# A two-layer decoder step in fp32 on one core: resident split weights, queued sums of x, rearranged decode

## The chip, the core and the metric

One core of a Trainium2 chip runs the whole step. Its engines are TensorE (PE in the profile; PEld is its weight load), VectorE (DVE), ScalarE (ACT), GpSimd (POOL) and SyncE (SP, which here only issues DMAs). The metric is the device time of one execution in microseconds (us), the median of the runs.

## The reference

One inference step of a small hybrid decoder, d_model 1024, 1024 prompt tokens and 8 decode tokens, feed-forward width 2816, 8 heads. Layer 0 mixes by a gated short convolution, layer 1 by differential attention (two softmaxes per head, one subtracted from the other) over keys and values of the prompt; the decode tokens also read 256 cached positions through a page table. Everything is fp32.

```python
def trunk(x, ...):
    for l in range(2):
        if l == 0:
            y = short_conv_mixer(x, conv_state, w_in, conv_w, w_mix_out)   # (b * conv(c * h)) @ w_out
        else:
            k, v = x @ w_kv          # rotary on k
            q = x @ w_q              # rotary on q
            o = diff_softmax_attention(q, k, v, ..., lam)   # softmax_1 - lam * softmax_2, times v
            y = (rms_norm(o, subln_g) * (1 - lam_init)) @ w_o
        x = layer_norm(alpha * x + y, ln1_g[l], ln1_b[l])
        x = layer_norm(alpha * x + (silu(x @ w_gate[l]) * (x @ w_up[l])) @ w_down[l], ln2_g[l], ln2_b[l])
```

## The kernel before

Tokens lie along the free dimension, d_model along the 128 partitions in 8 blocks. The 1032 tokens are four chunks of 258 (`HALF` = chunks (0, 1) and (2, 3)). An fp32 matmul is done as three products of rounded halves (hi by hi, lo by hi, hi by lo): `xhf` and `xlf` hold x so split, and a dense block of 128 outputs for one chunk (`dense`) is 24 matmuls of 128x258, eight at L299, eight at L300 and eight at L302.

Weights come from DRAM through a `Stream`: a DMA of 128x512 fp32 into `raw` (L134, on SP), a rounding copy to `whi` on ScalarE (L166), and `wlo` = raw - whi on GpSimd (L167). The ring has four split tiles and four raws; a second stream with 7 and 4 serves q and k. A pass that runs again over other chunks streams and splits its weights again.

Work off TensorE that belongs to a neighbouring stage (LayerNorms, sums of x, the decode) is written as generators on a side queue, `Side`; after each dense block a few steps of the front one are issued. `need(c)` drains the LayerNorm of chunk c where its result is wanted. A scheduler then orders each engine's instructions by its own priorities, so that the queues hold them in other orders than the code.

`layer_norm` (L327 to L367): mean by a matmul with ones (L327), subtraction of it (L338, two of 128x1032), squares on ScalarE (L343), their sum on VectorE (L335), variance by a matmul (L351, `st<-ssq`), square root on ScalarE (L353), reciprocal on VectorE (L354), multiplication (L358, two of 128x1032), scale and shift on ScalarE (L360), and the split into `xhf` (ScalarE, L365) and `xlf` (VectorE, L367). The next dense product of that chunk waits for the last two.

The FFN runs 11 groups of 256 hidden columns. The first is plain; groups 1 to 9 use a Winograd-like scheme with seven products of sums of weights and of sums of x (`sums_of`: `Th`, `Tl`, L318 and L319, called through `split_into`); the last is plain again, over chunks ((0, 1), (2, 3)) in layer 0 and (0, 1), (2), (3) in layer 1. `gate` (L470) and `up` (L478) fill `hidh`/`hidl`; `down` adds its products to the residual (L443, L445) and sums it for the next mean (L451).

After layer 0's FFN come q and k (8 blocks each, in two passes over two chunks; the stores of k are `out_k<-t`), v, and between them the decode: cached keys and values are gathered by indirect DMAs on GpSimd (L805), multiplied on VectorE (keys L827, L829; values L882, added in pairs L886) and, for values, summed over positions by `od` matmuls (L888). The softmax of the decode starts once chunk 3's keys are there (`k_done`). Then attention per head and block of queries loads k, q and v again from DRAM (`load`, `load_q`, `load_v`: L937 to L956) and takes scores at L969 and L970. The output projection is `project`, with four blocks of chunk 0 begun inside attention, in passes over chunks (0), (1, 2), (3).

## Time and profile before

| | |
|---|---|
| median of 3 runs | 2616.46 us (2613.49 to 2617.38) |
| profiled execution | 2614.26 us, span 2612.5 us |
| mean granted TensorE clock | 0.975 |
| PE busy | 2446.3 us, 94% of the span |
| DVE, POOL, ACT busy | 1502.9, 1315.0, 1015.1 us |

The busy time of an engine counts its instructions, not its waits. TensorE is busy for 94% of the span; the other engines are busy for 58% and less, unevenly. The granted clock is a share of full speed: 1.00 is 2.4 GHz and 0.5 is 1.2 GHz.

### The profile page before, as it was taken

Reading aid. Unit: us, or ns where it says so; the run is one execution under the profiler, and the core shown is the slowest. Engines: PE = TensorE matmul, PEld = TensorE weight load, DVE = VectorE, ACT = ScalarE, POOL = GpSimd, SP = SyncE. Lnnn points to the kernel's source line nnn. Section 1 sums busy time; section 2 is a strip of 40 time slices with the busy share of each in tenths; the row PEclk is TensorE's granted clock in tenths of the full one; section 3 lists DMA queues with packets and bytes.
Section 4 is the critical chain, followed back from the end, with each engine's and each line's share of the span. In section 5 each row is a group of like instructions: output and inputs, shape, how many; then the busy total and the mean of one; then the engine's idle time right before and its main releaser. Section 6 shows DMA issues by size and latency. Waiting matters only on the chain. (4 is left out here: it accounts for less than half of the span.)

```text
span 2612.5 us, 49681 instructions
## 1 busy us (share of the span) xinstructions
PE 2446.3 (94%) x19482; PEld 2381.7 (91%) x19482; DVE 1502.9 (58%) x2808; ACT 1015.1 (39%) x2248; POOL 1315.0 (50%) x1111
## 2 busy tenths in 40 slices
PE   9999998999999999989879899898799999999995
PEld 8999998999999999979849898797799999999984
DVE  4333878555555554594782677768654444444467
ACT  4213456322222222454322677646422222222234
POOL 4224576655555554465572244457555555555443
PEclk9999998999999999999989999999899999999997
DMA  4113242211111112267982768343211111111232
GB/s 158 49 45 93 82 139 84 63 49 50 53 50 49 49 49 86 90 224 225 290 281 92 194 179 242 107 140 106 77 57 50 49 49 49 50 50 49 82 94 97
DMA packets 158618, 266.16 MB, mean 102 GB/s; under 512 B 17672, under 2 KB 60072, under 8 KB 157232
## 3 DMA queue, kind: packets, MB, share of 16 engines
q1 hardware_dynamic: 151168, 236.01, 29.9%
q0 software_dynamic: 4608, 16.78, 1.8%
q10 hardware_dynamic: 2608, 10.20, 1.2%
q8 instruction: 153, 2.51, 0.4%
q14 instruction: 81, 0.66, 0.1%
HBM read 219.53 MB, written 43.39 MB: 101 GB/s over the span
## 5 line engine op out<-in xcount | busy, mean ns | idle before, releaser
L167 POOL TENSOR_TENSOR wlo<-raw,whi 128x512 fp32r<-128x512 f32 x570 | 773.2, 1369 | 760.6 <-ACT whi L166 496.2
L299 PE MATMUL mm<-xhf,whi 128*128 128x258 f32 x3200 | 809.9, 288 | 50.2 <-ACT xhf L365 19.8
L300 PE MATMUL mm<-xlf,whi 128*128 128x258 f32 x3200 | 804.1, 286 | 9.7 <-DVE xlf L367 9.0
L299 PEld LDWEIGHTS mm<-xhf,whi 128*128 128x128 f32 x3200 | 613.4, 192 | 60.7 <-ACT xhf L365 20.7
L300 PEld LDWEIGHTS mm<-xlf,whi 128*128 128x128 f32 x3200 | 614.2, 192 | 13.1 <-DVE xlf L367 10.4
L166 ACT CAST whi<-raw 128x512 fp32r<-128x512 f32 x570 | 349.5, 619 | 652.7 <-PE mm L300 499.0
L302 PE MATMUL mm<-xhf,wlo 128*128 128x258 f32 x3200 | 478.7, 285 | 4.0 <-POOL wlo L167 4.0
L302 PEld LDWEIGHTS mm<-xhf,wlo 128*128 128x128 f32 x3200 | 426.3, 191 | 5.7 <-POOL wlo L167 5.2
L299 PE MATMUL mm<-hidh,whi 128*128 128x258 f32 x1408 | 366.3, 288 | 14.6 <-DVE g L478 3.5
L300 PE MATMUL mm<-hidl,whi 128*128 128x258 f32 x1408 | 374.6, 286 | 2.8 <-DVE hidl L319 2.8
L302 PE MATMUL mm<-hidh,wlo 128*128 128x258 f32 x1408 | 282.8, 284 | 1.4 <-POOL wlo L167 1.4
L299 PEld LDWEIGHTS mm<-hidh,whi 128*128 128x128 f32 x1408 | 264.1, 190 | 19.2 <-DVE rf L445 5.3
L300 PEld LDWEIGHTS mm<-hidl,whi 128*128 128x128 f32 x1408 | 268.1, 191 | 6.4 <-DVE hidl L319 6.4
L167 POOL TENSOR_TENSOR wlo<-ws,whi 128x512 fp32r<-128x512 f32 x108 | 139.2, 1289 | 209.3 <-ACT whi L166 209.3
L299 PE MATMUL mm<-Th,whi 128*128 128x258 f32 x864 | 219.0, 285 | 4.7 <-DVE m L506 4.7
L302 PEld LDWEIGHTS mm<-hidh,wlo 128*128 128x128 f32 x1408 | 221.0, 192 | 1.6 <-POOL wlo L167 1.6
L300 PE MATMUL mm<-Tl,whi 128*128 128x258 f32 x864 | 217.4, 282 | 0.0
L445 DVE TENSOR_TENSOR rb<-mm,rb 128x258 f32<-128x258 f32 x320 | 134.6, 425 | 99.2 <-PE mm L302 99.1
L445 DVE TENSOR_TENSOR rf<-mm,rf 128x258 f32<-128x258 f32 x352 | 142.8, 422 | 68.7 <-PE mm L302 68.6
L299 PEld LDWEIGHTS mm<-Th,whi 128*128 128x128 f32 x864 | 163.9, 190 | 6.8 <-DVE m L506 6.5
L300 PEld LDWEIGHTS mm<-Tl,whi 128*128 128x128 f32 x864 | 163.6, 189 | 0.0
L166 ACT CAST whi<-ws 128x512 fp32r<-128x512 f32 x108 | 66.9, 620 | 229.9 <-PE mm L300 208.6
(221 smaller groups left out, 3717.7 us busy)
## 6 DMA issues: line engine op xcount, KB each, us to landing
raw<-in_wts SPq DMA_DIRECT2D x570, 256.0 KB
qh<-qh SPq DMA_DIRECT2D x64, 128.0 KB
ql<-ql SPq DMA_DIRECT2D x64, 128.0 KB
rf<-in_xT SPq DMA_DIRECT2D x16, 258.0 KB
stash<-rf SPq DMA_DIRECT2D x4, 1032.0 KB
qh<-hi SPq DMA_DIRECT2D x32, 129.0 KB
ql<-lo SPq DMA_DIRECT2D x32, 129.0 KB
out_k<-t SPq DMA_DIRECT2D x32, 129.0 KB
```

The costliest lines, as they stand in the source:

```text
L166: nc.scalar.copy(out=hi, in_=src)
L167: g.tensor_tensor(out=lo, in0=src, in1=hi.bitcast(F32), op=ALU.subtract)
L299: T.matmul(ps, lhsT=wh, rhs=h, start=(first and i == 0), stop=False, **kw)
L300: T.matmul(ps, lhsT=wh, rhs=l, start=False, stop=False, **kw)
L302: T.matmul(ps, lhsT=wl, rhs=h, start=False, stop=(last and i == len(terms) - 1), **kw)
L445: V.tensor_tensor(out=R[:, n], in0=ps, in1=R[:, n], op=ALU.add)
```

## The change

Four things. First, weights that a stage uses over several passes are split once and stay on chip (`Resident`): the output projection's eight blocks, in passes over single chunks, and of the last FFN group both gates, both ups and half of the downs, in the space of `T`, which is closed before it; layer 0's last group now has layer 1's order, and in both the first gate of chunk 3 goes ahead of chunk 2's downs. Second, the splits of the sums of x are queued behind the last LayerNorm's copies on ScalarE and VectorE, and the LayerNorm's reciprocal is written to PSUM. Third, the first two q blocks use the main stream, the second stream has 8 split tiles and 3 raws, and keys go over chunk 3 first and then over the other three; the decode's od products are issued one pair late, and its gathers behind them. Fourth, attention's first loads are issued on GpSimd.

```diff
+class Resident:
+
+    RAWS = 4
+
+    def __init__(self, nc, wts, pool, keys):
+        self.nc, self.wts, self.pool, self.keys, self.tiles = nc, wts, pool, keys, []
+        self.raws = deque()
+        self.loaded = 0
+        self._load()
+
+    def _load(self):
+        while len(self.raws) < self.RAWS and self.loaded < 2 * len(self.keys):
+            raw = self.pool.tile([P, 512], F32, tag="rraw", name="rraw", bufs=self.RAWS)
+            self.nc.sync.dma_start(out=raw, in_=self.wts[UIDX[self.keys[self.loaded // 2]], self.loaded % 2])
+            self.raws.append(raw)
+            self.loaded += 1
+
+    def get(self, key):
+        i = 2 * self.keys.index(key)
+        while len(self.tiles) < min(2 * len(self.keys), i + 6):
+            hi, lo = (self.pool.tile([P, 512], F32R, name=f"res{n}{len(self.tiles)}") for n in "hl")
+            raw = self.raws.popleft()
+            self.nc.scalar.copy(out=hi, in_=raw)
+            self.nc.gpsimd.tensor_tensor(out=lo, in0=raw, in1=hi.bitcast(F32), op=ALU.subtract)
+            self.tiles.append((hi, lo))
+            self._load()
+        return self.tiles[i:i + 2]
+
+
...
-    def pair():
+    def pair(key=None):
+
+        for res in kept.values():
+            if key in res.keys:
+                return res.get(key)
...
+    order = {}
...
-        V.reciprocal(out=ssq, in_=ssq)
+        V.reciprocal(out=var, in_=ssq)
...
-            V.tensor_tensor(out=v, in0=v, in1=ssq.unsqueeze(1).broadcast_to([P, KP, CH]), op=ALU.mult)
+            V.tensor_tensor(out=v, in0=v, in1=var.unsqueeze(1).broadcast_to([P, KP, CH]), op=ALU.mult)
...
+                order["A"] = A.copy(out=xh[c][:, ks], in_=v).ins
+                order["V"] = V.tensor_tensor(out=xl[c][:, ks], in0=v, in1=xh[c][:, ks].bitcast(F32),
+                                             op=ALU.subtract).ins
...
-                split_into(h[:, i], l[:, i], u)
+                with tc.issue_after(order["A"]), tc.issue_after(order["V"]):
+                    split_into(h[:, i], l[:, i], u)
...
+            blocks = pair(("down", l, g, i)) if ("down", l, g, i) in final else None
             for _ in range(2):
-                w = ws.take()
+                w = blocks[_] if blocks else ws.take()
...
-        def plain(g, chunks):
-            for f in (2 * g, 2 * g + 1):
-                block(half(("gate", l, f)), lambda f=f: gate(f, chunks))
-                block(half(("up", l, f)), lambda f=f: up(f, chunks))
+        final = [(n, l, f) for f in (NF - 2, NF - 1) for n in ("gate", "up")] + [("down", l, NG - 1, 0)]
+
+        def keep_final():
+            tpool.close()
+            kept["ffn"] = Resident(nc, wts, tpool.enter_context(tc.tile_pool(name="kept", bufs=1)), final)
+
+        def needs(*keys):
+            return half(*[k for k in keys if k not in final])
+
+        def plain(g, chunks, some=slice(0, 4)):
+            todo = [(n, f) for f in (2 * g, 2 * g + 1) for n in (gate, up)]
+            for n, f in todo[some]:
+                block(needs((n.__name__, l, f)), lambda n=n, f=f: n(f, chunks))
 
         def downs(g, chunks, ln=None):
             for i in range(2):
-                block(half(("down", l, g, i)), lambda i=i: down(g, i, chunks, ln))
+                block(needs(("down", l, g, i)), lambda i=i: down(g, i, chunks, ln))
 
...
+                block([], keep_final)
             downs(g, range(NCH))
-        for chunks in (((0, 1), (2,), (3,)) if l else HALF):
-            plain(NG - 1, chunks)
-            downs(NG - 1, chunks, (1, l, l == 1))
+        ln = (1, l, l == 1)
+        g = NG - 1
+        plain(g, (0, 1))
+        downs(g, (0, 1), ln)
+        plain(g, (2,))
+        plain(g, (3,), slice(0, 1))
+        downs(g, (2,), ln)
+        plain(g, (3,), slice(1, 4))
+        downs(g, (3,), ln)
 
 
...
+        def total(b):
+            for half in range(2):
+                T.matmul(od[half], lhsT=sel[:, b], rhs=vv[2 * b % 8][:, half * 512:(half + 1) * 512],
+                         start=(b == 0), stop=(b == DEC - 1))
+
         for j, (b, pg) in enumerate(pairs):
-            if j + ahead_v < 16:
-                gather(vv[(j + ahead_v) % 8], cache_v, *pairs[j + ahead_v])
             t = vv[j % 8].rearrange("p (h e) -> p h e", e=VD)
             V.tensor_tensor(out=t, in0=t, in1=at[:, pg, b].unsqueeze(2).broadcast_to([P, HEADS, VD]), op=ALU.mult)
             yield
             if pg:
                 t0 = vv[(j - 1) % 8]
                 V.tensor_tensor(out=t0, in0=t0, in1=vv[j % 8], op=ALU.add)
-                for half in range(2):
-                    T.matmul(od[half], lhsT=sel[:, b], rhs=t0[:, half * 512:(half + 1) * 512],
-                             start=(b == 0), stop=(b == DEC - 1))
+                if b:
+                    total(b - 1)
+                for i in range(j + 5, min(j + 7, 16)):
+                    gather(vv[i % 8], cache_v, *pairs[i])
                 yield "op"
+        yield "op"
+        total(DEC - 1)
         yield "op"
...
-        load(0)
-        load_q(0, 0)
-        load_v(0)
+        load(0, G)
+        load_q(0, 0, G)
+        load_v(0, G)
...
-            w = pair() if n not in begun or 0 not in chunks else None
+            w = pair(("o", n)) if n not in begun or 0 not in chunks else None
...
-        for chunks in ((0,), (1, 2), (3,)):
+        for c in range(NCH):
             for n in range(KT):
-                block([] if 0 in chunks and n < BEGIN else half(("o", n)), lambda n=n, chunks=chunks: f(n, chunks))
+                block([], lambda n=n, c=c: f(n, (c,)))
 
 
...
-        open_pools(stack, ("big", 1, {}), ("m", 8, {}), ("g", 2, {}))
+        nonlocal tpool
+        open_pools(stack, ("hid", 1, {}), ("m", 8, {}), ("g", 2, {}))
+        pools["hid"] = [pools["hid"].tile([P, 2, NCH, CH], F32R, name=f"hid{n}") for n in "hl"]
+        tpool = stack.enter_context(ExitStack())
+        open_pools(tpool, ("big", 1, {}))
         pools["T"] = [pools["big"].tile([P, 2, 3, KP, CH], F32R, name=f"T{n}") for n in "hl"]
-        pools["hid"] = [pools["big"].tile([P, 2, NCH, CH], F32R, name=f"hid{n}") for n in "hl"]
 
...
-    produce("k", (HALF[1], HALF[0]))
+    early_q, part_q = part_q[:2], part_q[2:]
+    produce("k", ((3,), (0, 1, 2)))
...
+            run(early_q)
+            ws = Stream(nc, wts, pools["wb"], items(part_q, part_k), 8, 3)
...
-        ffn_space(ph)
         rb = pools["r"].tile([P, NCH, KT, CH], F32, name="rb")
         for c in range(NCH):
             r[c] = rb[:, c]
         reload(None)
+        with ExitStack() as pw:
+            open_pools(pw, ("wo", 1, {}))
+            kept["o"] = Resident(nc, wts, pools["wo"], [("o", n) for n in [*range(BEGIN, KT), *range(BEGIN)]])
+            run(part_o)
+        kept.clear()
+        ffn_space(ph)
```

VectorE in layer 0, where the last LayerNorms of the convolution mixer meet the sums of x. The first piece is the kernel before; `Tl` is the low half of a sum of x, `ssq` the sum of squares and later its square root, `st` the mean in PSUM.

```order
L335 TENSOR_TENSOR ssq<-ssq,t 128x258
L319 TENSOR_TENSOR Tl<-m,Th 128x258
L451 TENSOR_TENSOR sum<-sum,rf 128x258
L319 TENSOR_TENSOR Tl<-m,Th 128x258 x7
L354 RECIPROCAL ssq<-ssq 128x258
L319 TENSOR_TENSOR Tl<-m,Th 128x258 x2
L338 TENSOR_TENSOR rf<-rf,st 128x1032 x2
L358 TENSOR_TENSOR rf<-rf,ssq 128x1032 x2
L319 TENSOR_TENSOR Tl<-m,Th 128x258 x2
```

The same place of the changed kernel, on VectorE, and, after the cut, the row at which the last LayerNorm ends and what follows it.

```order
L373 TENSOR_TENSOR ssq<-ssq,t 128x258
L491 TENSOR_TENSOR sum<-sum,rf 128x258
L392 RECIPROCAL st<-ssq 128x258
L376 TENSOR_TENSOR rf<-rf,st 128x1032 x2
L396 TENSOR_TENSOR rf<-rf,st 128x1032 x2
...
L405 TENSOR_TENSOR xlf<-rf,xhf 128x4x258 x2
L354 TENSOR_TENSOR Tl<-m,Th 128x258 x3
```

The `Tl` splits have left the place ahead of chunk 2's reciprocal and chunk 3's subtraction of the mean, and stand behind the last copies of chunk 3.

TensorE in layer 1, from the variance of chunk 3's LayerNorm (`st<-ssq`) to the gate of chunk 3 (`mm<-xhf` just behind it before the change). First the kernel before.

```order
L302 MATMUL mm_22605<-xhf,wlo 128x258 x8
L351 MATMUL st<-ssq,cs 128x258
L299 MATMUL mm<-xhf,whi 128x258
L299 MATMUL mm_22605<-xhf,whi 128x258
L300 MATMUL mm<-xlf,whi 128x258
```

The changed kernel on TensorE, from the same product on: the blocks `mm_22178` (24 matmuls), `mm_22179` (24), `mm` (chunk 2's gate, 24) and `mm_22450` (24), and then chunk 3's gate in the last two rows.

```order
L389 MATMUL st<-ssq,cs 128x258
L334 MATMUL mm_22178<-xhf,whi 128x258
...
L337 MATMUL mm_22178<-xhf,wlo 128x258 x8
...
L337 MATMUL mm_22179<-xhf,wlo 128x258 x8
...
L337 MATMUL mm<-xhf,wlo 128x258 x8
...
L337 MATMUL mm_22450<-xhf,wlo 128x258 x8
L334 MATMUL mm<-xhf,whi 128x258
L335 MATMUL mm<-xlf,whi 128x258
```

Before, no matmul stands between the variance and chunk 3's gate; now 96 do.

SyncE's DMA queue just ahead of attention, before the change: stores of v, and the first loads of k (`tk`), q (`qh`, `ql`) and v (`tv`).

```order
L739 DMA out_v<-dec_v 8x256
L736 DMA out_v<-vt 128x256 x7
L937 DMA tk<-kh 64x1024
L736 DMA out_v<-vt 128x256
L938 DMA tk<-kl 64x1024
L937 DMA tk<-kh 64x1024
L938 DMA tk<-kl 64x1024
L950 DMA qh<-qh 64x512 x2
L950 DMA ql<-ql 64x512 x2
```

The same loads after the change, on GpSimd, behind the last weight splits and the decode's scaling.

```order
L167 TENSOR_TENSOR wlo<-raw,whi 128x512 x12
L974 TENSOR_SCALAR ss<-ss 8x8
L975 TENSOR_TENSOR ss<-ss,mhalf 8x8
L1001 DMA tk<-kh 64x1024
L1002 DMA tk<-kl 64x1024
L1001 DMA tk<-kh 64x1024
L1002 DMA tk<-kl 64x1024
L1014 DMA qh<-qh 64x512 x2
L1014 DMA ql<-ql 64x512 x2
```

The thirteen loads have moved from SyncE's queue to GpSimd's, where nothing else stands between them.

## Rows read from the trace of the kernel before

**Rows 1.** The page, group five: busy, mean, then idle before it and why.

```profile
L299 PE MATMUL mm<-xhf,whi 128*128 128x258 f32 x3200 | 809.9, 288 | 50.2 <-ACT xhf L365 19.8
```

**Rows 2.** Windows, PE: length, busy (matmuls), granted clock, DMA share, GB/s.

```profile
200.00:240.00 40.00, 40.00 (x336) 1.00 0.33 93
400.00:440.00 40.00, 28.53 (x201) 0.83 0.24 73
1120.00:1160.00 40.00, 29.87 (x204) 0.87 0.72 241
1280.00:1320.00 40.00, 32.09 (x248) 0.91 1.00 347
1840.00:1880.00 40.00, 28.27 (x190) 0.76 0.26 80
2560.00:2600.00 40.00, 23.21 (x143) 0.79 0.25 86
```

**Rows 3.** Timeline of DVE, 388 to 396 us, LayerNorms of chunks 2 and 3.

```profile
388.99 5.16 DVE L319 TENSOR_TENSOR Tl<-m,Th 128x258 fp32r<-128x258 f32 x7
394.07 1.75 DVE L354 RECIPROCAL ssq<-ssq 128x258 f32<-128x258 f32 x1
```

**Rows 4.** Timeline of PE, 405 to 440 us.

```profile
426.90 0.80 PE L299 MATMUL mm<-xhf,whi 128*128 128x258 f32 x2 [8.35 <-ACT xhf L365]
```

**Rows 5.** Timeline of PE, 1837 to 1849 us.

```profile
1837.18 0.70 PE L351 MATMUL st<-ssq,cs 128*128 128x258 f32 x2 [1.11 <-DVE ssq L335]
1848.15 0.80 PE L299 MATMUL mm<-xhf,whi 128*128 128x258 f32 x2 [10.27 <-ACT xhf L365]
```

**Rows 6.** Timeline of PE, 1688 to 1722 us.

```profile
1703.33 0.36 PE L299 MATMUL mm<-xhf,whi 128*128 128x258 f32 x1 [1.97 <-DVE xlf L1046]
```

**Rows 7.** Timeline of PE, 1100 to 1180 us.

```profile
1123.35 0.60 PE L351 MATMUL st<-ssq,cs 128*128 128x258 f32 x2
1130.04 0.58 PE L299 MATMUL mm<-xhf,whi 128*128 128x258 f32 x1 [6.09 <-ACT whi L166]
1137.33 0.51 PE L299 MATMUL mm<-xhf,whi 128*128 128x258 f32 x2 [1.18 <-ACT xhf L365]
```

**Rows 8.** Lines L358 and L338: durations min/median/max in ns, first and last start.

```profile
L358 DVE TENSOR_TENSOR rf<-rf,ssq x16: 1216/1232/2324, 304.9 to 1184.0; 128x1032 f32<-128x1032 f32 x16
...
L338 DVE TENSOR_TENSOR rf<-rf,st x16: 1215/1222/1230, 289.0 to 1169.7; 128x1032 f32<-128x1032 f32 x16
```

**Rows 9.** Timeline of PE and ACT, 1280 to 1362 us.

```profile
1295.74 0.58 PE L299 MATMUL mm<-xhf,whi 128*128 128x258 f32 x1 [5.71 <-ACT whi L166]
1336.03 3.57 PE L888 MATMUL od<-rf,sel 128*8 128x512 f32 x4 [10.46 <-DVE rf L886]
...
1294.76 0.41 ACT L318 CAST hi<-t 128x258 fp32r<-128x258 f32 x1 [9.17 <-DMA out_k<-t]
```

**Rows 10.** Timeline of DVE, 1324 to 1334 us.

```profile
1324.58 5.22 DVE L882 TENSOR_TENSOR rf<-rf,at 128x1024 f32<-128x1024 f32 x3
1332.40 1.21 DVE L886 TENSOR_TENSOR rf<-rf 128x1024 f32<-128x1024 f32 x1
```

**Rows 11.** Timelines of SP, POOL and PE about the first loads of attention.

```profile
1432.77 0.51 SPq L937 DMA_DIRECT2D tk<-kh  x1
1437.09 1.23 SPq L950 DMA_DIRECT2D ql<-ql  x2
...
1286.80 0.96 POOL L805 DMA_INDIRECT rf<-in_cache_k,idx  x1 [0.16 <-DVE dec_k L680]
...
1443.49 0.55 PE L969 MATMUL S<-tk,qh 128*128 128x256 f32 x1 [5.78 <-DMA ql<-ql]
```

**Rows 12.** Timeline of PE, 2535 to 2612 us.

```profile
2544.57 0.39 PE L299 MATMUL mm<-hidh,whi 128*128 128x258 f32 x1 [3.49 <-DVE g L478]
2575.56 0.39 PE L299 MATMUL mm<-hidh,whi 128*128 128x258 f32 x1 [1.93 <-ACT whi L166]
2591.90 1.20 PE L412 MATMUL st<-sum,cs 128*128 128x258 f32 x2 [5.74 <-DVE sum L451]
```

23 lines of the change are left out of this document (12 added, 11 removed).

## The prediction

> **What bounds the kernel now.** I read the page's list of costly groups first. A matmul of a dense product is recorded at 288 ns because matmuls are pipelined; the largest cause of PE's idle time before such a line is the ScalarE copy of a LayerNorm's result, xhf [rows 1]. Then I cut the span into 40-us windows. An undisturbed window holds 336 matmuls, so one costs 40/336 = 0.119 us, and each matmul missing from a window of dense products is 0.119 us lost. Most windows are full, so nothing that merely saves work on another engine can be gained there. The losses stand where one stage ends and the next begins: 16.1 us in 400 to 440 (135 matmuls missing), 15.7 in 1120 to 1160, 10.5 in 1280 to 1320, 17.4 in 1840 to 1880, 23.0 in 2560 to 2600 [rows 2]. Part of each is waiting and part a lower granted clock behind the wait: in 1840 to 1880 PE was idle for 40 - 28.27 = 11.7 us, so the other 5.7 us of the loss is slow matmuls at a mean clock of 0.76 [rows 2]. I then read, for each of these places, what PE waited for in its timeline.
>
> **The change, part by part.**
>
> *O projection into FFN1.* Before, the mean-square product of chunk 3's LayerNorm starts at 1837.18 and the gate of chunk 3 is the very next work on PE; it starts at 1848.15, after 10.27 us of waiting for xhf [rows 5]. So the chain from the variance to xhf takes 10.97 us, all uncovered. The new project() goes chunk by chunk, so chunks 1 and 2 are normalised earlier, and the order of PE shows 96 matmuls between that same product and the gate of chunk 3: 96 x 0.119 = 11.4 us of cover. Covered work on VectorE and ScalarE gets into the chain, though (gates and ups of chunks 0 to 2). I take a remaining wait of 2 us: 9 us gained, and 5 of the 5.7 us of slow clock and smaller waits about it. Term: 14 us gained; bounds 6 (chain lengthened to 17 us) and 17.4 (the whole loss of that window).
>
> *Convolution mixer into FFN0.* Before, VectorE does seven Tl splits for 5.16 us ahead of the reciprocal of chunk 2's LayerNorm [rows 3], and everything of chunk 3's LayerNorm queues behind it; PE then waits 8.35 us for chunk 3's xhf [rows 4]. After, all Tl splits stand behind the last LayerNorm's copies, so this chain begins 5 us earlier. What is late next: the splits themselves, needed only by the first FFN group of sums, a full pass of gate and up later. PE reaches the gate no earlier, so at most 8.35 us and the slow clock behind it (16.1 - 11.5 idle = 4.6 us) can go. Term: 6 gained; bounds 3 (ScalarE, which the splits also leave, was not in the way) and 12.
>
> *LayerNorm's reciprocal in PSUM.* The product with the reciprocal reads PSUM instead of SBUF. The same shape with a PSUM operand (L338) never takes over 1.23 us; with an SBUF operand (L358) the median is the same and the longest 2.32 [rows 8]. So it is worth nothing at the median and up to 1.1 us per instruction where something is in the way. It is already in the terms of the chains.
>
> *FFN0 into q.* Before, PE waits 6.09 us for the first weights of a stream whose buffers become free only with the last FFN matmul, then 1.18 us for xhf of chunk 1; that arrives at 1137.33, 14.0 us after the variance product at 1123.35 [rows 7]. After, the first two q blocks come from the main stream, whose weights are there. But chunk 0's 24 matmuls cover 2.9 us of the 14, and chunk 1's first matmul stands next on PE, ahead of chunk 0's second block. The same chain then ends the same stall. Term: 2 gained; bounds -2 and 6 (the weights' wait).
>
> *Keys and decode.* The od products wait 10.46 us [rows 9]: five multiplications by the softmax are issued on VectorE ahead of the first addition that od needs, at 5.22/3 = 1.74 us each, and the addition takes 1.21 [rows 10]. After, four stand ahead and about 40 matmuls (4.8 us) stand on PE between the softmax's transposition and the first od pair; the second group of three pairs, 18 matmuls later, again waits for three more pairs. I sum 4 x 1.2 + 1.2 + 0.5 - 4.8 = 2 us for the first and about 6 for the second: 2 to 3 us gained. Against it: the first key pass now has one chunk, so it needs two weight tiles of 256 KB per 24 matmuls (2.86 us) where it had 48, in a stretch where the DMA share is 1.00 at 347 GB/s [rows 2]. The 5.71 us that PE waited there for whi came from a ScalarE queue held 9.17 us by an out_k transfer [rows 9]; the later pass of three chunks asks for less. Term: 4 gained; bounds -10 (that wait twice more) and 10.5 (the window's loss).
>
> *Attention's first loads, from SP to POOL.* Before, SP issues the first tk at 1432.77 and the eighth load it needs ends its issue at 1438.32: 0.6 us each, one store among them; the first scores start at 1443.49 after 5.78 us of waiting [rows 11]. In the new order the first load waits for the same matmul, so it cannot start earlier. No plain load issued by POOL is in the trace; the nearest row is a gather, 0.96 us [rows 11]: 8 x 0.96 = 7.7 us, 2 us later than SP. Term: 2 lost; bounds 0 (landing, not issue, sets the end) and 5 lost (all 13). The Trainium skill, "DMA: Bandwidth & Descriptors", Specifications and "SWDGE vs HWDGE vs iDMA", puts the first byte of a GpSimd-issued DMA at about 1 us and of one from SP at about 0.6, and says plain loads belong on SP: by that 8 x 0.4 = 3.2 us would be lost here and the sum come out 1.2 us worse. No row here shows a plain load issued by POOL, so the trace neither bears it out nor contradicts it.
>
> *O projection's start.* The resident weights lie where attention's tiles lay, and their first load waits for the last transposition of attention, the matmul just ahead of the first that needs them. Before, the stream was already full and PE only waited 1.97 us, until 1703.33, for xlf [rows 6]. The nearest row of a cold start is the 6.09 us above [rows 7]: 1701.36 + 6.1 = 1707.5, so 4.1 later. Term: 4 lost; bounds 2 and 8. That 32 fewer splits follow in the later passes is hidden beneath PE's full windows and worth nothing.
>
> *FFN's last group and the end.* The gate of chunk 3 ahead of chunk 2's downs puts 24 matmuls (2.9 us) over a wait of 3.49 us, and the resident weights take away 1.93 [rows 12]. But in the new order chunk 1's normalisation ends only beside the last matmuls, so two products of 1.2 and a reciprocal of 1.75 [rows 3, 8] move to the queue ahead of chunk 3's sums, for which PE waits 5.74 [rows 12]. Term: 3 gained; bounds -2 and 7.
>
> Sum: 14 + 6 + 2 + 4 - 2 - 4 + 3 = 23 us. The profiled execution took 2614.26 us with a span of 2612.5, 2.2 below the median of the runs; 2616.5 - 23 = 2593.
>
> **The rivals.**
> *The chains take the stall's place* (20%). LayerNorm's chain is limited by VectorE, whose queue holds the same work in another order; the wait for chunk 3's xhf would come back elsewhere. For it: the sums of squares, splits and multiplications still have to run on it in the same 40 us. Against it: 96 matmuls of cover. Then the two first terms shrink to their lower bounds, 6 + 3 instead of 20: 12 us gained in all, less the 4 that the decode may not give: 8, 2608.
> *The key pass is bound by DMA* (14%, slower). In its one-chunk pass: 16 weight tiles of 256 KB (4.2 MB), some ten gathers and five broadcasts of 512 KB (7.9 MB), 24 stores of 129 KB (3.2 MB), 15.3 MB at the 347 GB/s that the window shows [rows 2] is 44 us against 8 x 24 x 0.119 = 22.9 us of matmuls. If none of it is loaded ahead or let run behind, PE waits 21 us and runs at a lower clock afterwards, about 6: 27 lost instead of 4 gained, 2593 + 31 = 2624. It decides from about 23 + 4 = 27 us lost in this pass. Against it: most weights of the pass are in the ring before it begins, and before the change the same crowding cost 10.5 us.
> *All chains covered* (11%). The upper bounds of the first two terms and of the end: 17.4 + 12 + 7 instead of 23 adds 13: 2580, and down to 2570 where the keys' window empties too.
>
> **How the numbers follow.** 55% for the sum above, whose own range is 2580 to 2606 (the terms' bounds taken as independent). The other cases reach from 2570 to 2624; leaving out the outer half of the first and most of the slower one, 2570 to 2616 holds 8 in 10. A measurement of this kernel tells about 0.2%, 5.2 us, from no change. Faster: 55 + 11 + 10 of the 20 of the stalled case: 76%. The same: the rest of that, 10%, and 1 of the slower case: 11%. Slower: 13%.
>
> **What would show it.** Right: no wait of 8 us or more for xhf at the gate of chunk 3 in either FFN; a wait for a resident weight of some 4 to 6 us at the first o projection matmul; the first scores no earlier after the last v product than now; an xhf wait of about 10 us at the second q product. Wrong: a new wait for whi or wlo in the first key pass of over 10 us in all; a wait for Tl or Th in the first group of sums; chunk 3's final sum more than 6 us after the last down product.

## The result and the profile after

The changed kernel takes 2587.52 us (median of 4 runs, 2584.38 to 2593.24) against 2615.97 for the kernel before, run beside it: ratio 0.9895 (95% interval 0.9875 to 0.9914, in brackets from here on), so 28.5 us faster where 23 were forecast. The profiled executions compare in the same way, span 2582.6 against 2612.5 us. The two kernels have the same 19482 matmuls, so the n-th of each can be set side by side. This ledger is made of their start times, in us from the start of the span, in one trace of each.

| stretch (n-th matmul) | before, us | after, us | gained | forecast |
|---|---|---|---|---|
| to 4000: convolution mixer, start of FFN0 | 513.6 | 513.1 | 0.6 | 6 |
| to 8700: FFN0 | 1084.2 | 1085.2 | -1.5 | 0 |
| to 9350: FFN0's last group, first q blocks | 1183.7 | 1186.8 | -2.1 | 2 |
| to 10700: q, keys, decode | 1387.9 | 1389.3 | 1.6 | 4 |
| to 12000: start of attention | 1567.1 | 1577.5 | -8.9 | -2 |
| to 12750: attention | 1685.4 | 1694.3 | 1.5 | 0 |
| to 12900: start of the output projection | 1706.6 | 1720.2 | -4.8 | -4 |
| to 14200: output projection into FFN1 | 1906.8 | 1888.7 | 31.8 | 14 |
| to 18700: FFN1 | 2467.4 | 2449.9 | -0.7 | 0 |
| to the last: FFN1's last group and the end | 2599.6 | 2569.2 | 12.9 | 3 |

The sum is nearly right, but six of its seven terms are not. A stretch differs from trace to trace even where no edit touches it: over the kernels below, from the 9350th to the 10700th matmul by -2.2 to 2.0 us against the kernel before, from the 12900th to the 14200th by 29.7 to 31.8. Differences of two or three us between single traces tell nothing.

The page's line of the commonest product, and then PE in windows (length, busy, matmuls, granted clock, DMA share, GB/s), as in [rows 1, 2]:

```profile
L334 PE MATMUL mm<-xhf,whi 128*128 128x258 f32 x2720 | 686.3, 287 | 40.3 <-ACT xhf L403 20.5
```

```profile
1320.00:1360.00 40.00, 27.77 (x159) 0.83 0.72 250
1440.00:1480.00 40.00, 26.65 (x158) 0.79 0.73 175
1760.00:1800.00 40.00, 40.00 (x330) 1.00 0.08 28
1800.00:1840.00 40.00, 39.39 (x325) 1.00 0.29 86
1840.00:1880.00 40.00, 34.58 (x261) 0.96 0.23 73
```

Two windows of the kernel before that belong beside them:

```profile
1760.00:1800.00 40.00, 35.96 (x287) 1.00 0.47 143
1800.00:1840.00 40.00, 28.60 (x200) 0.90 0.24 74
```

and the longest wait in them, from PE's timeline:

```profile
1821.79 0.58 PE L299 MATMUL mm<-xhf,whi 128*128 128x258 f32 x1 [4.41 <-ACT g L470]
```

The three windows from 1760 held 287, 200 and 190 matmuls [rows 2]; after, the first two are full and the third has 261. That is the gain. 1440 to 1480 held 233 before and holds 158: attention's first scores wait longer. In 1120 to 1160, with 204 before [rows 2] and 210 after, little has changed. What PE waits for most after, in total (times, longest):

```profile
PE mm L334 <- ACT xhf L403: 20.5, 2, 11.9
PE mm L337 <- POOL wlo L167: 13.7, 2, 11.7
```

Of the waits for xhf the one of 10.27 us at FFN1's gate [rows 5] is gone, the one at FFN0's gate has stayed, and the one at q has grown from 1.18 [rows 7] to 11.89. One of 11.67 for wlo is new, and the first scores wait 8.13 instead of 5.78 [rows 11]. Where they stand on PE's timeline (start, length, instruction, then in brackets the wait and its releaser; from seven places of the trace):

```profile
424.27 0.80 PE L334 MATMUL mm<-xhf,whi 128*128 128x258 f32 x2 [8.64 <-ACT xhf L403]
...
454.34 0.39 PE L334 MATMUL mm<-hidh,whi 128*128 128x258 f32 x1 [1.85 <-DVE rf L483]
...
1137.65 0.80 PE L334 MATMUL mm<-xhf,whi 128*128 128x258 f32 x2 [11.89 <-ACT xhf L403]
...
1341.50 1.66 PE L337 MATMUL mm<-xhf,wlo 128*128 128x258 f32 x6 [11.67 <-POOL wlo L167]
...
1447.30 0.55 PE L1033 MATMUL S<-tk,qh 128*128 128x256 f32 x1 [8.13 <-issue]
1454.26 0.55 PE L1034 MATMUL S<-tk,ql 128*128 128x256 f32 x1 [3.58 <-DMA ql<-ql]
...
1715.12 0.58 PE L334 MATMUL mm<-xhf,resh 128*128 128x258 f32 x1 [4.87 <-ACT resh L203]
...
2558.87 0.99 PE L389 MATMUL st<-ssq,cs 128*128 128x258 f32 x2 [3.59 <-DVE ssq L373]
2568.63 1.23 PE L464 MATMUL st<-m,cs 128*128 128x258 f32 x2 [7.91 <-DVE m L462]
```

*FFN0's gate of chunk 3* waits 8.64 us, as before (8.35, [rows 4]). The variance product ahead of it starts at 413.00 after and 415.60 before, so the chain from there to xhf takes 11.3 us in both. ScalarE and VectorE show what it consists of:

```profile
414.35 1.28 ACT L391 ACT_TABLE_LOAD   x1
415.64 0.48 ACT L391 ACTIVATE ssq<-st,eps_t 128x258 f32<-128x258 f32 x1
...
419.23 4.05 ACT L398 ACTIVATE rf<-rf,prm_t 128x258 f32<-128x258 f32 x8 [1.41 <-DVE rf L396]
...
416.15 1.77 DVE L392 RECIPROCAL st<-ssq 128x258 f32<-128x258 f32 x1 [1.16 <-ACT ssq L391]
417.96 2.37 DVE L396 TENSOR_TENSOR rf<-rf,st 128x1032 f32<-128x1032 f32 x2
```

A table load, the square root, the reciprocal, a multiplication, eight scalings and a copy: each waits for the one before it, and no split of sums stands among them. Moving the splits let this chain start 2.6 us earlier and did not shorten it. Nor did the start hold: at the 3400th matmul the changed kernel is 3.6 us ahead of the kernel before, and between the 3500th and the 3525th, in FFN0's first downs, it gives 2.9 back. The downs wait there for VectorE's additions to the residual (1.85 us above, none before), and the moved splits stand in VectorE's queue among them:

```profile
451.38 1.17 DVE L354 TENSOR_TENSOR xlf<-m,xhf 128x258 fp32r<-128x258 f32 x1
```

The kernel below whose splits are not queued has no such wait there.

*The second q product* waits 11.89 us; only chunk 0's 24 matmuls of the first q block stand on PE while chunk 1's chain runs. VectorE is busy for 19.86 of the 20 us from 1120 to 1140, and ScalarE, which needs 4.2 us to scale the chunk, stands in its queue behind copies of weights that have not landed:

```profile
1128.97 1.93 ACT L166 CAST whi<-raw 128x512 fp32r<-128x512 f32 x3 [2.79 <-DMA raw<-in_wts]
1130.81 2.08 ACT L398 ACTIVATE rf<-rf,prm_t 128x258 f32<-128x258 f32 x4
```

*The od products* no longer show a wait for VectorE [rows 9], but the dense product ahead of them waits 11.67 us for a wlo, and VectorE has finished by then. POOL has that split behind a gather, and the gather stands there while VectorE multiplies and adds:

```profile
1330.63 9.53 POOL L862 DMA_INDIRECT rf<-in_cache_v,idx  x1 [5.96 <-DVE rf L947]
1340.18 1.27 POOL L167 TENSOR_TENSOR wlo<-raw,whi 128x512 fp32r<-128x512 f32 x1
...
1338.11 1.21 DVE L947 TENSOR_TENSOR rf<-rf 128x1024 f32<-128x1024 f32 x1
```

VectorE's last addition ends at 1338.11 + 1.21 = 1339.32, and the gather at 1330.63 + 9.53 = 1340.16, 0.84 later. Before, the gather at this place took 8.39 us, but four splits had been made between it and the gather ahead of it, not two, and PE waited for a split only 2.79 us:

```profile
1333.88 8.39 POOL L805 DMA_INDIRECT rf<-in_cache_v,idx  x1 [6.30 <-DVE rf L886]
```

*Attention's first loads*, now on POOL (start, length, instruction, wait and releaser):

```profile
1434.45 0.64 POOL L1001 DMA_DIRECT2D tk<-kh  x1 [14.92 <-PE vps L788]
1440.75 0.52 POOL L1014 DMA_DIRECT2D qh<-qh  x1 [2.03 <-DMA tk<-kh]
1442.18 0.52 POOL L1014 DMA_DIRECT2D qh<-qh  x1 [0.91 <-DMA tk<-kl]
1445.93 0.52 POOL L1014 DMA_DIRECT2D ql<-ql  x1 [1.21 <-DMA tk<-kl]
```

Issuing one takes 0.52 to 0.64 us, about as long as on SP (0.51, and 1.23 for two, [rows 11]). But the ninth to twelfth each wait until one of the first four has landed, and SP, free meanwhile, sends loads for later blocks past them.

### The profile page after: what moved, and what is told of

It reads as the page before. It is cut to its first block, busy times and chain, and to the rows that moved or that the text cites. A ratio compares the mean times of both kernels' runs of the same rounds, so it can differ in the third digit from the quotient of the medians.

```text
span 2582.6 us, 49334 instructions
## 1 busy us (share of the span) xinstructions
PE 2435.3 (94%) x19482; PEld 2374.2 (92%) x19482; DVE 1457.1 (56%) x2808; ACT 981.6 (38%) x2194; POOL 1233.4 (48%) x1072
## 5 line engine op out<-in xcount | busy, mean ns | idle before, releaser
L167 POOL TENSOR_TENSOR wlo<-raw,whi 128x512 fp32r<-128x512 f32 x482 | 643.7, 1344 | 689.1 <-ACT whi L166 516.7
L334 PE MATMUL mm<-xhf,whi 128*128 128x258 f32 x2720 | 686.3, 287 | 40.3 <-ACT xhf L403 20.5
L335 PE MATMUL mm<-xlf,whi 128*128 128x258 f32 x2720 | 682.3, 285 | 1.4 <-DVE xlf L354 0.8
L334 PEld LDWEIGHTS mm<-xhf,whi 128*128 128x128 f32 x2720 | 520.2, 191 | 47.5 <-ACT xhf L403 20.9
L335 PEld LDWEIGHTS mm<-xlf,whi 128*128 128x128 f32 x2720 | 520.4, 191 | 4.1 <-issue 1.7
L166 ACT CAST whi<-raw 128x512 fp32r<-128x512 f32 x482 | 296.4, 619 | 592.0 <-PE mm L335 406.0
L337 PE MATMUL mm<-xhf,wlo 128*128 128x258 f32 x2720 | 409.4, 285 | 13.7 <-POOL wlo L167 13.7
L337 PEld LDWEIGHTS mm<-xhf,wlo 128*128 128x128 f32 x2720 | 364.1, 192 | 16.8 <-POOL wlo L167 14.2
L334 PE MATMUL mm<-hidh,whi 128*128 128x258 f32 x1344 | 350.5, 286 | 12.9 <-DVE g L518 2.3
L335 PE MATMUL mm<-hidl,whi 128*128 128x258 f32 x1344 | 355.1, 285 | 1.7 <-DVE hidl L354 1.3
```

Source lines behind the costliest of these rows:

```text
L166: nc.scalar.copy(out=hi, in_=src)
L167: g.tensor_tensor(out=lo, in0=src, in1=hi.bitcast(F32), op=ALU.subtract)
L334: T.matmul(ps, lhsT=wh, rhs=h, start=(first and i == 0), stop=False, **kw)
L335: T.matmul(ps, lhsT=wh, rhs=l, start=False, stop=False, **kw)
L337: T.matmul(ps, lhsT=wl, rhs=h, start=False, stop=(last and i == len(terms) - 1), **kw)
```

## The experiments

All are timed beside the kernel before; stage times are taken from one trace of each, as in the ledger. Kernels not said to differ are the changed kernel with one edit.

**Attention's first loads back on SP.**

```diff
-        load(0, G)
-        load_q(0, 0, G)
-        load_v(0, G)
+        load(0)
+        load_q(0, 0)
+        load_v(0)
```

> The changed kernel with attention's first thirteen loads given back to SP. In the changed kernel's trace each of POOL's plain loads takes 0.53 to 0.64 us to issue, no more than SP's 0.6, but the ninth to twelfth wait 2.03, 0.91, 1.51 and 1.21 us for the landing of the first four, while SP sends loads for later heads past them; PE waits 8.13 us for the first scores and 3.58 us for the next query tile. Theory A (that wait in POOL's queue, and SP's later loads let through, cost the 6 us which the profile lost here): back on SP the waits are about 5.8 and 0.4 us as before, the time is 2582 us, ratio to before 0.987. Rival B (issue on POOL costs 2 us, as predicted): 2585.5 us, ratio 0.9884. Rival C (bandwidth sets the end of these loads on either engine): 2587.5 us, ratio 0.9891 to 0.9895, and a wait of 8 us again.

Measured: 2582.43 us, ratio 0.9862 [0.9845, 0.9879]. The first scores wait for loads by SP:

```profile
1449.01 0.55 PE L1033 MATMUL S<-tk,qh 128*128 128x256 f32 x1 [6.39 <-DMA ql<-ql]
```

From the 11000th to the 12000th matmul this kernel loses 0.7 us against the kernel before. The changed kernel loses 9.2 there; in the seven kernels below that keep POOL's loads, 7 to 13. Theory A holds, and the edit makes the kernel faster: the interval just touches that of the changed kernel, but the stage shows it, and a kernel below with the same loads has 0.9861. Whether POOL's waits or the loads that pass them cost the time was not separated.

**The order of the projection alone**, in the kernel before:

```diff
-        for chunks in ((0,), (1, 2), (3,)):
+        for chunks in ((0,), (1,), (2,), (3,)):
```

> The kernel before with one edit: the output projection's passes take chunks 0, 1, 2, 3 one at a time instead of 0, (1, 2), 3; the weights are streamed and split anew in each pass. Theory A (the order alone covers the LayerNorm chains, since two splits of 1.34 us on POOL just fit into 24 matmuls of 2.86 us): no wait over 3 us for xhf at the gate of chunk 3, and 20 to 31 us less: 2585 to 2596 us, ratio 0.988 to 0.992. Rival B (residency is what pays: with a pair of tiles for every 24 matmuls the splits on POOL and the copies on ScalarE, which the LayerNorms need too, become the bound of the passes): the wait for xhf goes, waits for wlo and whi take its place, and under 10 us are gained: 2606 to 2617 us, ratio 0.996 to 1.000.

Measured: 2615.93 us, ratio 0.9992 [0.9983, 1.0001]. The long wait for xhf at the gate of chunk 3 is gone, as the order should make it, and other waits have come (the last row is POOL's window):

```profile
1762.02 0.39 PE L299 MATMUL mm<-xhf,whi 128*128 128x258 f32 x1 [3.00 <-ACT whi L166]
...
1817.52 0.55 PE L299 MATMUL mm<-xhf,whi 128*128 128x258 f32 x1 [5.78 <-DVE rb L443]
...
1760.00:1800.00 40.00, 36.13 (x30) 0.91 0.55 153
```

At the 13550th matmul it is 29.7 us behind the kernel before, and by the 14200th it has made up 26 of them. POOL, which splits the weights and makes the sums of x, is busy for 36.13 of 40 us (32.00 before). Rival B holds: order alone is worth nothing.

**Residency without the order**, the old passes from the resident weights:

```diff
-        for c in range(NCH):
+        for chunks in ((0,), (1, 2), (3,)):
             for n in range(KT):
-                block([], lambda n=n, c=c: f(n, (c,)))
+                block([], lambda n=n, chunks=chunks: f(n, chunks))
```

> The changed kernel with its output projection in the old passes, chunk 0, then 1 and 2 together, then 3, from the resident weights. Theory A (the order covers the chains): the wait of about 10 us for xhf at the gate of chunk 3 returns, with the smaller ones before it, and 10 to 20 us of the 31 gained between the first o product and FFN1 are lost again: 2598 to 2608 us, ratio 0.993 to 0.997. Rival B (residency, which frees POOL and ScalarE, is what shortens the chains): at most 6 us lost, 2588 to 2594 us, ratio 0.989 to 0.9915.

Measured: 2610.05 us, ratio 0.9964 [0.995, 0.9978].

```profile
1853.78 0.80 PE L334 MATMUL mm<-xhf,whi 128*128 128x258 f32 x2 [8.38 <-ACT xhf L403]
```

The wait is back, and from the 12900th to the 14200th matmul 13.3 us are gained on the kernel before instead of 31.8. This kernel also keeps the queued splits; the order alone, without them and without resident weights, gives 0.5 there (4.1 us behind at the 12900th matmul, 3.6 at the 14200th). So the order adds 18.5 us where the weights are resident and nothing where they are streamed: theory A is right only with residency. Residency with neither the order nor the queued splits was not run.

**What of the stream is it that residency takes away?** Spare work on one engine, with no weights behind it; for ScalarE the last line is `A.copy(out=spare, in_=two)`:

```diff
                 add_product(c, n, begun[n] if w is None else dense(mm(), w, c), True, True)
                 side.step(RATE)
+                if c and 0 < n < KT - 1:
+                    two = r[c][:, n - 1:n + 1]
+                    for _ in range(2):
+                        spare = pools["wo"].tile([P, 2, CH], F32, tag="spare", name="spare", bufs=1)
+                        G.tensor_tensor(out=spare, in0=two, in1=two, op=ALU.subtract)
```

> The changed kernel, with work added that nothing needs: in the output projection's passes over chunks 1, 2 and 3, after each of the blocks 1 to 6, POOL makes two subtractions of 128x516 from SBUF to a spare tile, 36 in all, about as many and as long as the weight splits that a streamed pass would make there (1.3 us each). No DMA, no ScalarE work and no weight comes with them. Theory A (residency pays because VectorE's instructions with both operands in SBUF wait out POOL's instructions that read SBUF): the additions sum<-sum,rb, 441 ns on average from 1740 to 1850 us in the changed kernel and 874 before, rise to 700 ns or more, those that read PSUM stay at 420 and 1220 ns, the LayerNorm chains lengthen, waits come back between 1760 and 1850 us, and 5 to 18 us are lost: 2592 to 2606 us, ratio 0.991 to 0.996. Rival B (it is the stream's DMA, or the waits for weights themselves): the means stay within 10%, at most 2 us lost, ratio 0.989 to 0.9905.

> The same, with the 36 spare pieces of work given to ScalarE as copies of 128x516 (about 0.62 us each, 22 us in all) instead of POOL. Theory A (the conflict is between VectorE and POOL): VectorE's means do not move, ScalarE has room, at most 3 us lost, ratio 0.989 to 0.991. Rival C (ScalarE's queue, where the copies whi of a streamed pass stand among the LayerNorm's activations, is what residency frees): VectorE's means do not move, but 5 us or more are lost, ratio 0.991 or more.

Measured: with POOL 2593.60 us, ratio 0.9896 [0.9877, 0.9915]; with ScalarE 2592.57 us, ratio 0.9896 [0.9876, 0.9916]; both as the changed kernel. VectorE's instructions from 1740 to 1850 us (count, busy, mean ns of one), in the changed kernel, with POOL's spare work, with ScalarE's:

```profile
L491 DVE TENSOR_TENSOR sum<-sum,rb 128x258 f32<-128x258 f32 x18 | 7.9, 441 | 0.4
```

```profile
L491 DVE TENSOR_TENSOR sum<-sum,rb 128x258 f32<-128x258 f32 x18 | 15.7, 872 | 0.4
L396 DVE TENSOR_TENSOR rb<-rb,st 128x1032 f32<-128x1032 f32 x8 | 9.4, 1220 | 0.0
```

```profile
L491 DVE TENSOR_TENSOR sum<-sum,rb 128x258 f32<-128x258 f32 x19 | 9.7, 509 | 0.4
```

Half of theory A is shown, half falls. An addition with both operands in SBUF doubles, 441 to 872 ns (874 before the change), when POOL reads SBUF beside it, and does not follow ScalarE (509); a product with one operand in PSUM stays at 1220. The Trainium skill has this rule ("SBUF — State Buffer", Who interferes with whom: a VectorE instruction with two SBUF inputs contends with a GpSimd instruction that reads SBUF), and these rows agree with it. But no wait came back from 1760 to 1850 and the stretch gained 31.9 us as without the spare work: the order has cover enough for the longer chains. With ScalarE's work it gained 29.4, hardly outside the spread between traces (29.7 to 31.8). Neither is what makes a streamed pass slow by itself; whether it is both together, or the waits for the weights, stays open.

**The last FFN group without resident weights**, its new order kept (the line that makes the `Resident` goes too):

```diff
-        final = [(n, l, f) for f in (NF - 2, NF - 1) for n in ("gate", "up")] + [("down", l, NG - 1, 0)]
+        final = []
```

> The changed kernel with no weights of the last FFN group kept on chip, in both FFNs; the order of its blocks stays. The last 130 us of the changed kernel gained 15 us. Theory A (the order of the blocks gives most of it; the resident weights were priced at the 1.93 us that PE waited for whi): 2 to 4 us lost, 2590 to 2592 us, ratio 0.990 to 0.991. Rival B (with one chunk for each pair of tiles the stream is at its limit, and residency gives most of it): waits for whi or wlo of 5 us or more in each FFN's last group, 8 to 20 us lost, 2596 to 2608 us, ratio 0.992 to 0.997.

Measured: 2610.05 us, ratio 0.9966 [0.9953, 0.9979]. Rival B holds by size, but not by the wait that it named: little of it is for whi.

```profile
1124.78 0.80 PE L335 MATMUL mm<-hidl,whi 128*128 128x258 f32 x2 [4.42 <-DVE hidl L354]
1130.00 0.58 PE L334 MATMUL mm<-hidh,whi 128*128 128x258 f32 x1 [3.13 <-DVE g L518]
```

PE waits for VectorE, in whose queue the additions take 1059 ns from 1085 to 1130 us against 580 in the changed kernel. At FFN0's end (8700th to 9350th matmul) this kernel loses 17.2 us to the kernel before, the changed one 2.1; at FFN1's end it gains 6.5, the changed one 12.9. So residency is worth 15 and 6.3 us, and what FFN0's end gets of it is needed to pay for the new order of its blocks.

**The splits of the sums not queued behind the LayerNorms** (without the orders that `issue_after` imposes, the edges):

```diff
-                with tc.issue_after(order["A"]), tc.issue_after(order["V"]):
-                    split_into(h[:, i], l[:, i], u)
+                split_into(h[:, i], l[:, i], u)
```

> The changed kernel without the edges that queue the splits of sums of x behind the LayerNorms' last copies. Between its convolution mixer and FFN0 the changed kernel gained only about 0.5 us where 6 were forecast; the chain from the last variance product to chunk 3's xhf takes 11.3 us in both kernels (413.0 to 424.3 against 415.6 to 426.9). Theory A (this chain, on which the splits do not stand, sets the end; the edges move only its start by 2 to 3 us): within 4 us of the changed kernel, 2584 to 2591 us, ratio 0.988 to 0.991, and the chain again 11.3 us. Rival B (the splits, let through, now delay the chunk-by-chunk LayerNorms of FFN1 too, where the edges are worth what was forecast): 6 to 12 us lost, ratio 0.9917 to 0.994.

Measured: 2599.90 us, ratio 0.9923 [0.9907, 0.994]. At FFN0's start the edges prove to be worth 1 to 2 us (9.54 us of waiting for xhf instead of 8.64), no more than single traces differ by; from the 12900th to the 14200th matmul this kernel gains 22.8 us instead of 31.8, with these waits there:

```profile
1828.32 0.58 PE L334 MATMUL mm<-xhf,whi 128*128 128x258 f32 x1 [4.58 <-ACT g L509]
```

Rival B holds: the edges matter, at the second place and not at the first. A wait for ScalarE's g is what the kernel before had at the second place too (4.41 us); that the edges pay there because the chunks' LayerNorms are spread beside the splits is read from the order and not tried by itself.

**All q blocks in the second stream:**

```diff
-    early_q, part_q = part_q[:2], part_q[2:]
+    early_q, part_q = part_q[:0], part_q
```

> The changed kernel with the first two q blocks back in the new phase's own stream. Between FFN0 and q the changed kernel lost about 3 us where 2 were forecast as gained: chunk 1's xhf comes 17.2 us after the last variance product, 14.0 before, and ScalarE, which must scale and copy it, waits 2.79 and 0.55 us in its queue for raw weight tiles. Theory A (these copies stand in ScalarE's queue among the LayerNorm's activations whichever stream they belong to; the early blocks only move the wait from whi to xhf): 2584 to 2591 us, ratio 0.988 to 0.991, with a wait of about 6 us for whi and less than 8 for xhf. Rival B (the early blocks pay, the loss comes from the last FFN group's new order): 4 to 8 us lost, 2592 to 2596 us, ratio 0.991 to 0.9925.

Measured: 2590.32 us, ratio 0.9883 [0.9862, 0.9905].

```profile
1127.88 0.58 PE L334 MATMUL mm<-xhf,whi 128*128 128x258 f32 x1 [5.00 <-ACT whi L166]
1136.06 0.50 PE L334 MATMUL mm<-xhf,whi 128*128 128x258 f32 x2 [2.66 <-ACT xhf L403]
```

Theory A: 5.00 and 2.66 us of waiting in place of 11.89, the stretch within 1.3 us. The early blocks change the name of the wait.

**Keys and od as before**, in the changed kernel with its new ring (passes of the keys `(HALF[1], HALF[0])`; the gather of tile j + 6 ahead of product j, and the od products straight behind their addition):

> The changed kernel with the passes of the keys in halves and the decode's od products and gathers as they were before; the stream keeps 8 split tiles and 3 raw ones. Theory A (the rearrangement gave about 1 us there: the 10.46 us that PE waited for VectorE's sums turned into 11.67 us of waiting for a split behind a gather on POOL): 2586 to 2590 us, ratio 0.988 to 0.991, and the od products wait about 10 us again. Rival B (the forecast of 4 us was right and hidden by losses elsewhere): 2591 to 2594 us, ratio 0.991 to 0.993. Rival C (the one-chunk pass of the keys costs more than it gives, DMA being at its limit): 2578 to 2584 us, ratio 0.985 to 0.9875.

Measured: 2600.74 us, ratio 0.9926 [0.9912, 0.9939]: rival B by the ratio, and more than it said by the stage. From the 9350th to the 10700th matmul this kernel loses 9.0 us to the kernel before, where the changed one gains 1.6. Its waits there:

```profile
1302.10 0.56 PE L904 MATMUL sp<-cs,wide 128*128 128x1 f32 x2 [9.67 <-DVE wide L900]
...
1343.57 3.57 PE L938 MATMUL od<-rf,sel 128*8 128x512 f32 x4 [6.16 <-DVE rf L949]
```

So the rearrangement (keys and od together) is worth 10.6 us by these two traces, more than the 4 forecast, and with the old order and the new stream the stage is worse than it was before. Something else in it takes 9 us away. The early q blocks do not (0.9 us gained here without them); the one other edit in this stage is the stream's.

**The stream with 7 split and 4 raw tiles**, and attention's first loads on SP:

```diff
-            ws = Stream(nc, wts, pools["wb"], items(part_q, part_k), 8, 3)
+            ws = Stream(nc, wts, pools["wb"], items(part_q, part_k), 7, 4)
```

> The changed kernel with attention's first loads on SP (2582.4 us, ratio 0.9862), and the stream of q, keys and v with 7 split and 4 raw tiles, as before the change, instead of 8 and 3. The old order of keys and od lost some 10 us inside the changed kernel, although the changed kernel gained only about 1 us over the kernel before in that stage, so something else in it lost some 8 us; the size of the ring is the other edit there. Theory A (with three raw tiles the loads start later and PE waits for whi and wlo in the first key pass, 1.30, 0.27, 0.46 and 2.08 us): these waits go, and 3 to 8 us are gained: 2574 to 2579 us, ratio 0.983 to 0.985. Rival B (DMA, at a share of 1.00 there, sets when weights land, whatever the ring): within 2 us, ratio 0.9855 to 0.987.

Measured: 2567.96 us, ratio 0.9816 [0.9802, 0.983]: 51.2 us less than the kernel before, beyond what was expected. From the 9350th to the 10700th matmul it gains 12.2 us; the changed kernel with the same loads loses 1.0. Not where theory A looked: the waits for whi in the first key pass are still there (0.60, 0.41, 2.09). The wait of 11.67 us is gone. POOL's queue shows why:

```profile
1321.96 2.54 POOL L167 TENSOR_TENSOR wlo<-raw,whi 128x512 fp32r<-128x512 f32 x2
1325.63 1.64 POOL L167 TENSOR_TENSOR wlo<-raw,whi 128x512 fp32r<-128x512 f32 x1 [1.13 <-ACT whi L166]
1329.13 1.52 POOL L167 TENSOR_TENSOR wlo<-raw,whi 128x512 fp32r<-128x512 f32 x1 [1.85 <-ACT whi L166]
1334.34 8.39 POOL L862 DMA_INDIRECT rf<-in_cache_v,idx  x1 [3.69 <-DVE rf L947]
```

The gather still stands 8.39 us, from 1334.34 to 1342.73, and VectorE's last addition ends at 1341.89, 0.84 earlier again. But with the old ring four splits are made ahead of it instead of two, and PE works from them meanwhile: from 1320 to 1360 it has 249 matmuls at a clock of 0.97 instead of 159 at 0.83. Which of the ring's two numbers does it was not separated. This is the version that beats both kernels.

**The reciprocal in SBUF**, again with the loads on SP:

```diff
-        V.reciprocal(out=var, in_=ssq)
+        V.reciprocal(out=ssq, in_=ssq)
...
-            V.tensor_tensor(out=v, in0=v, in1=var.unsqueeze(1).broadcast_to([P, KP, CH]), op=ALU.mult)
+            V.tensor_tensor(out=v, in0=v, in1=ssq.unsqueeze(1).broadcast_to([P, KP, CH]), op=ALU.mult)
```

> The changed kernel with attention's first loads on SP (2582.4 us, ratio 0.9862), and the LayerNorm's reciprocal in SBUF again. With it in PSUM the products that use it take 1220 ns on average between 1740 and 1850 us, with it in SBUF 1682 in the kernel before and 1483 in the one with a streamed projection; two such products stand in each LayerNorm's chain. Theory A (an SBUF operand more makes them wait for POOL): these products take 1400 ns or more where POOL works, the three uncovered chains become about 0.5 to 2 us longer each, and 2 to 5 us are lost: 2584 to 2587 us, ratio 0.987 to 0.988. Rival B (the waits were in time that is covered): within 1 us, ratio 0.986 to 0.9865.

Measured: 2581.70 us, ratio 0.9861 [0.9845, 0.9877], the same as without the edit. The products take up to 2323 ns, 1226 at the median, against 1230 and 1222: rival B.

**Four repairs together**: attention's first loads on SP, the first key tile and its queries ahead of the second, and the three edits below, where `ws.split` is the last split made and `pools["wr"]` is opened before attention (the first eight gathers, not six, are now issued at once):

```diff
-                        side.step(RATE if g == 0 else 1)
+                        side.step(RATE if g == 0 else 1 if ln is None else 3)
...
-                for i in range(j + 5, min(j + 7, 16)):
-                    gather(vv[i % 8], cache_v, *pairs[i])
+                with tc.issue_after(ws.split):
+                    for i in range(max(8, j + 3), min(j + 5, 16)):
+                        gather(vv[i % 8], cache_v, *pairs[i])
...
+    res_o = Resident(nc, wts, None, [("o", n) for n in [*range(BEGIN, KT), *range(BEGIN)]], pools["wr"])
```

> The changed kernel with five edits at places that the traces show apart. One: attention's first loads on SP, the first key tile and its queries ahead of the second. Two: the gathers that refill the decode's value tiles are queued on POOL behind the latest weight split and two tiles later; in the changed kernel the first of them stood on POOL from 1330.63 for 9.53 us while VectorE multiplied and added without a pause until 1339.3, and the split that PE waited 11.67 us for stood behind it. Three: in an FFN's last group each down product steps the LayerNorms by three pieces instead of one, since chunk 1's variance product comes only at 1120.41, with FFN0 nearly done, and PE then waits 11.89 us for its xhf. Four: the first four raw tiles of the resident output weights have their buffers from before attention (PE waited 4.87 us there). Theory A (each wait is where the trace puts it): 5 us and 2 from the first edit, 5 from the second (the next split still stands behind a gather), 8 from the third, 3 from the fourth: 23 less than 2587.5, 2564 us, ratio 0.980; the waits named shrink to at most half. Rival B (VectorE's and POOL's queues are the limit at the second and third place and the waits only change their names): 9 less, 2578 us, ratio 0.9855.

Measured: 2585.22 us, ratio 0.9865 [0.9848, 0.9882], no better than the loads on SP alone.

```profile
1138.42 0.80 PE L335 MATMUL mm<-xhf,whi 128*128 128x258 f32 x2 [11.86 <-ACT xhf L404]
...
1339.24 1.88 PE L939 MATMUL od<-rf,sel 128*8 128x512 f32 x4 [3.30 <-DVE rf L948]
```

More steps do not start chunk 1's chain earlier (its variance product is at 1121.21, at 1120.41 without): VectorE is full there, which is rival B. The held gathers take the wait of 11.67 us away, but the od products then wait 3.30 and a split 2.15, and the stretch gains 1.3 us. The fourth edit works: up to the first o products (12750th to 12900th matmul) this kernel loses 1.4 us where the changed one loses 4.8 and the one with its loads on SP 5.7. What it gains is lost at the start of attention, 6.4 us from the 10700th to the 12000th matmul against 0.4 with the plain loads on SP. The scores start after a wait of 3.97 us and then stop twice (3.99, 2.65). SP issues the four early raw tiles, 1 MB, from 1440.87 to 1442.64, between the first key tile's queries and the second key tile; whether they or the new order of the loads cost it stays open.

## Why the prediction came out right, point by point

The total was right to 5.5 us by luck: two terms that were much too small (o projection into FFN1 and the end, 27.7 us together) met four that were too favourable (18.9 us together). What was right is the place of the largest gain and its mechanism. By its steps:

- **O projection into FFN1: 14 forecast, 31.8 measured, above the bound of 17.4.** The mechanism holds: no wait for xhf is left at the gate of chunk 3 (0.61 us for xlf, where 2 were allowed for), and residency and order are both needed. The bound was wrong because it was read off one window: the "whole loss" of 1840 to 1880. The two windows ahead of it lacked 49 + 136 of their 336 matmuls, 22 us, and most of those came back as well (6 and 11 are missing after). Part of the gain, 9 us, is the edges on the splits of the sums, which the prediction counted elsewhere.
- **Conv into FFN0: 6 forecast, 0.6 measured.** The step that failed: "this chain begins 5 us earlier". The splits stood ahead of chunk 2's reciprocal, but the wait is chunk 3's, behind a variance product that moved by 2.6 us. The statement that no wait of 8 us would be left in either FFN is wrong here (8.64). And the moved splits were said to be needed only a full pass later; they are, but until then they stand in VectorE's queue ahead of the additions that the first downs need, and 2.9 of the 3.6 us gained by then went there.
- **FFN0 into q: 2 forecast, 2.1 lost.** The wait for xhf at the second q product came as stated (about 10, measured 11.89). The size failed: the chain is 17.2 us long instead of 14.0, and the last group's new order costs here what its residency gives. ScalarE's copies of weights that have not landed account for part of the 3.2 us: behind the first product with the reciprocal they hold the scaling up by about 1.7 us, where before the like waits lay ahead of that product; the rest is queueing on VectorE and ScalarE.
- **Keys and decode: 4 forecast, 1.6 measured.** The wait of od went, where 2 and about 6 us were forecast to stay. What the step missed is that with the ring's new size a gather stands ahead of a needed split on POOL: over this stage, with the old ring the old order stands at 0 and the new one at 12.2 gained, with the new ring at 9.0 lost and between 2.2 lost and 2.0 gained. The rearrangement is worth 7 to 12 us, and the ring takes 9 to 13. The key pass itself is not bound by DMA: its waits for whi and wlo add up to 4.1 us, so the slower rival fell.
- **Attention's first loads: 2 lost forecast, 8.9 measured, beyond the bound of 5.** Issue on POOL was priced, and is cheap (0.53 us). The waits for landing behind the first eight loads, and the loads that pass them, were not thought of. The Trainium skill's advice ("DMA: Bandwidth & Descriptors", "SWDGE vs HWDGE vs iDMA") to keep plain loads on SP is borne out by these runs (ratio 0.9862 on SP, 0.9895 on GpSimd); the 3.2 us made of its figures for the first byte is not.
- **O projection's start: 4 lost forecast, 4.8 measured**, with the wait of 4.87 us for a resident weight that was stated.
- **The end: 3 forecast, 12.9 measured.** The residency was priced at the 1.93 us of waiting for whi, and is worth 6.3: the term left out what else the streamed splits hold up. POOL's splits beside VectorE's additions are the likely part, argued and not shown. Ahead of chunk 3's last sums PE waits 3.59 us, for a variance, where it waited 5.74 [rows 12]; the queue that was feared there came one step later, between these sums and the last variance (chunk 2's reciprocal and two products), where PE waits 7.91 us instead of 5.94:

```profile
2599.03 1.20 PE L424 MATMUL st<-m,cs 128*128 128x258 f32 x2 [5.94 <-DVE m L422]
```

- **The reciprocal in PSUM** is worth nothing to the time, as stated for the median product.
- **The rivals.** The chains did not take the stall's place in FFN1 and did in FFN0 and at q; all chains covered (2580) was nearer at the end than in the middle. The time lies between that case and the forecast, 5.5 us from 2593.

## What to carry to other kernels

Before moving work out of a chain's way, find the last event that starts the chain whose end is waited for: what stands ahead of another chunk's chain moves its start and not its length, and a stall behind a last chain only goes by cover. Then look at what the moved work stands ahead of in its new place. Read the loss of a stage off all its windows, not off the one with the longest wait. When a ring, a pool or an issuing engine changes, look at what the new order puts ahead of the next needed weight on the in-order queues: here a ring of 7 split and 4 raw tiles instead of 8 and 3 was worth 12 us, and thirteen loads on the other queue 9.

## What the runs showed of the hardware

- A gather issued on GpSimd while VectorE runs instructions with both operands in SBUF back to back stays on its queue until VectorE stops. In all fourteen traces the longest gather began in such a run and ended 0.83 to 0.84 us after VectorE's last instruction, whatever its length (8.39 us in the kernel before, 9.53 in the changed one, 6.12 to 9.53 over all); the median gather takes 0.96 to 1.12. That this is the same contention as that of the 441 and 872 ns is argued from these coincidences, not tried by itself.
- A plain load issued by GpSimd takes about the issue time of one by SP (0.52 to 0.64 us against some 0.6), yet thirteen of them cost some 9 us. The ninth to twelfth wait there until one of the first four has landed (2.03, 0.91, 1.51 and 1.21 us), and SP's later loads pass them; which of the two costs the time was not separated.
- GpSimd's reads beside VectorE doubled VectorE's additions (441 to 872 ns) without costing the kernel anything in the stretch where that was tried: it gained 31.9 us with them and 31.8 without.
